# Layer-norm sums on GpSimd: who adds up z and its squares, and who subtracts the mean

## The chip, the cores and the metric

The kernel runs on one core of a Trainium2 chip. The metric is the device time of one execution in microseconds (us); the time before is the median of three executions. The core's engines appear in the profile as PE (TensorE matmuls; PEld its weight loads), DVE (VectorE), ACT (ScalarE), POOL (GpSimd) and SP (SyncE). Each engine works through its own queue in a fixed order; they wait for each other with semaphores.

## What is computed

One inference step of a two-layer decoder trunk, for 256 prompt tokens and 8 sample tokens. In each layer three mixers (retention, a Mamba-2 SSD, sliding-window attention) read the same x, are merged with gates, and go through an output projection; then a SwiGLU FFN. Each half ends in a DeepNorm residual with a layer norm, and it is these norms that the change touches:

```python
def _layer_norm(x, g, b):
    mu = jnp.mean(x, -1, keepdims=True)
    var = jnp.mean(jnp.square(x - mu), -1, keepdims=True)
    return (x - mu) * lax.rsqrt(var + EPS) * g + b

# in each of the DEPTH = 2 layers, D_MODEL = 1024
mix = (g_a * br_a + g_b * br_b + g_c * br_c) @ w_out
x = _layer_norm(ALPHA * x + mix, ln1_g, ln1_b)                 # "norm 1"
ffn = (silu(x @ w_ffn_gate) * (x @ w_ffn_up)) @ w_ffn_down
x = _layer_norm(ALPHA * x + ffn, ln2_g, ln2_b)                 # "norm 2"
```

## The kernel before

**Layout.** All activations stand with channels on the partitions: the 1024 channels are 8 blocks of 128 (KB = 8), and a block is a tile of 128 partitions x 264 columns (T = 264, the 256 + 8 tokens). A projection is a row of units; one unit is one block of 128 output channels, made in one PSUM bank from K = 8 blocks of input.

**Products in three parts.** Full fp32 products are made from fp32r halves: every tensor has a high part and a low part, and for each pair of blocks TensorE multiplies wh by xh, wh by xl and wl by xh (mm3). A unit with K = 8 is so 24 matmuls. The weights arrive as raw strips by DMA on SP's queue and are split here (wsplit, L196): ScalarE copies wh, VectorE subtracts wl = raw - wh (both on 128 x 1024). There are three buffers each of wh and wl, so the splits can be a little ahead of the matmuls.

**The norms.** There are four: norm 1 of layer 0, norm 2 of layer 0, norm 1 of layer 1, and norm 2 of layer 1, which is the last one, has its own code in output() and is not changed ("final"). For block m, residual() makes z[m] from the PSUM result and the high and low part of x in two VectorE steps (the rows z<-xh,ps and z<-xl,z); from block 0 a per-token shift is formed that a matmul with the matrix neg puts into the later blocks. Then residual() does four things with z[m]: VectorE adds it to s1, the sum over blocks (tile s in the rows); ScalarE squares it (sq); the square goes into the sum of squares; and ScalarE and VectorE make the high and low part of g*z (xh and xl) for the next gemm. The sum of squares is kept in two ways. In norm 2 VectorE adds sq to a tile named sums. In norm 1 no such tile is given (sums is None), and TensorE takes every square at once: a product of the 128x128 ones matrix with sq, gathered over eight blocks in the PSUM tile ps_var. Since the matrix is all ones, the product also sums over the 128 partitions and spreads the result to all of them.

ln_stats() finishes the statistics: where sums is given, one product of ones with sums into ps_var; always one product of ones with s1 into ps_mu. ScalarE makes nmu (minus the mean) and the square of the mean, VectorE the variance (the row ps_var<-ps_var,rstd), ScalarE the square root and VectorE the reciprocal: rstd. ln_finish() then normalizes z for all blocks: VectorE adds nmu to z in four steps of two blocks (128x528), scales it by g and rstd, and ScalarE and VectorE make the new high and low part of x.

**What follows a norm.** The next gemms don't wait for ln_finish(). The first 8 units behind a norm run on g*z, not yet normalized (unnormed(), tile ps_z); their results are corrected afterwards by VectorE with nmu, rstd and two more columns of the same gemm (the rows v<-nmu,wc,ps_z). So TensorE can go on while the statistics and the normalized x are being made. Behind norm 1 these are the gemms of FFN blocks f = 0 to 3 (gate and up; w_fg, w_fu); the fifth FFN block is the first to read the normalized x. Behind norm 2 they are layer 1's attention projections (w_qc, w_v and others). The instruction mu_mm, the mean's product, is a mark: the scheduler may not put the later ones of these gemms ahead of it.

**What sets the order.** The code is written against a tile framework with a scheduler that simulates a timeline and decides each engine's order from readiness, priorities (high_priority, for the weight splits and the corrections) and "not before" marks (issue_after). A change of one instruction can so move others on every engine. GpSimd has almost no arithmetic; its queue carries software DMAs (dma(), ld(): parameters, the mixers' states, caches, bias tables) and a few memsets.

## Time and profile before

| what | value |
|---|---|
| time, median of 3 executions | 1091.47 us (1088.8 to 1091.77) |
| the profiled execution's own time | 1088.66 us |
| span of its profile | 1086.9 us |
| PE (TensorE) busy | 1068.3 us, 98% |
| DVE (VectorE) busy | 840.1 us, 77% |
| ACT (ScalarE) busy | 662.4 us, 61% |
| POOL (GpSimd) busy | 163.4 us, 15% |

The profiled execution is one of the kernel's own executions; its span is the time from its first to its last recorded instruction, and 1.8 us of its time lie around that. All times of single instructions are in us from the start of this span. Matmuls are pipelined: a record of 0.28 us starts 0.12 us after the one before it, so the cost of a matmul in a full queue is the distance of starts, not its duration. In a list of waits, a line names the waiting engine with its tile, the engine and tile that released it, and then the sum in us, the number and the mean. In a timeline, what stands in brackets behind a row is the idle time of its engine just before it and who ended it.

In this profile the w_o units of norm 1 in layer 0 run from 331 to 346 us, and the gemms behind it from 347 us on; norm 2 of layer 0 ends near 547 us; norm 1 of layer 1 near 876 us.

### The profile page before, as it was taken

Reading aid. Unit: us, or ns where it says so; the run is one execution under the profiler, and the core shown is the slowest. Engines: PE = TensorE matmul, PEld = TensorE weight load, DVE = VectorE, ACT = ScalarE, POOL = GpSimd, SP = SyncE. Lnnn points to the kernel's source line nnn. Section 1 sums busy time; section 2 is a strip of 40 time slices with the busy share of each in tenths; the row PEclk is TensorE's granted clock in tenths of the full one; section 3 lists DMA queues with packets and bytes.
Section 4 is the critical chain, followed back from the end, with each engine's and each line's share of the span. In section 5 each row is a group of like instructions: output and inputs, shape, how many; then the busy total and the mean of one; then the engine's idle time right before and its main releaser. Section 6 shows DMA issues by size and latency. Waiting matters only on the chain.

```text
span 1086.9 us, 22192 instructions
## 1 busy us (share of the span) xinstructions
PE 1068.3 (98%) x8619; PEld 1029.9 (95%) x8619; DVE 840.1 (77%) x1904; ACT 662.4 (61%) x1332; POOL 163.4 (15%) x248
## 2 busy tenths in 40 slices
PE   9999999999999999999999999999999999999998
PEld 7988998999999999999999899889999999999996
DVE  3588885898868997777599888478886899877654
ACT  3476556667646776665467855366675558666452
POOL 3300012522001011221020001153100000222300
PEclk9999999999999999999999999999999999999999
DMA  9854555994455678899675344669855546989951
GB/s 313 258 175 153 158 145 180 246 273 164 155 194 156 219 247 287 290 312 317 198 254 171 127 156 128 194 160 301 247 183 174 176 149 207 291 286 298 324 183 41
DMA packets 176826, 230.74 MB, mean 212 GB/s; under 512 B 8040, under 2 KB 151984, under 8 KB 176544
## 3 DMA queue, kind: packets, MB, share of 16 engines
q1 hardware_dynamic: 156384, 166.95, 47.6%
q0 software_dynamic: 20272, 62.34, 19.6%
q8 instruction: 68, 1.11, 0.4%
q14 instruction: 38, 0.31, 0.1%
q10 hardware_dynamic: 64, 0.03, 0.0%
HBM read 213.52 MB, written 19.61 MB: 214 GB/s over the span
## 4 chain that ended last, share of the span: by engine, by line
PE 61%; issue 26%; DMA 6%; DVE 3%; POOL 2%; ACT 1%; POOLq 0%; DVEq 0%; ACTq 0%
PE ps_gate L125 12%; PE ps_fg L125 10%; PE ps_fu L125 10%; PE ps_br L125 7%; PE ps_fd L125 6%; PE ps_z L125 5%; PE ps_o L125 4%; PE ps_u L125 4%; DMA bias<-bias_row 2%; DMA rs<-in_state_ret_dram 1%; PE ps_y L125 1%; DVE wl L146 1%; DMA vb<-scr_v 1%; PE ps_var L125 1%; DMA out_dram<-sn 1%
## 5 line engine op out<-in xcount | busy, mean ns | idle before, releaser
L125 PE MATMUL ps_u<-xh,wh 128*128 128x264 f32 x608 | 176.1, 291 | 3.1 <-ACT wh L141 1.8
L125 PE MATMUL ps_u<-xl,wh 128*128 128x264 f32 x608 | 176.4, 290 | 0.0
L125 PE MATMUL ps_u<-xh,wl 128*128 128x264 f32 x608 | 175.6, 291 | 0.1
L125 PEld LDWEIGHTS ps_u<-xh,wh 128*128 128x128 f32 x608 | 116.1, 192 | 6.5 <-ACT wh L141 2.3
L125 PEld LDWEIGHTS ps_u<-xh,wl 128*128 128x128 f32 x608 | 116.5, 192 | 2.1 <-issue 1.7
L125 PEld LDWEIGHTS ps_u<-xl,wh 128*128 128x128 f32 x608 | 116.3, 191 | 1.1 <-issue 0.5
L125 PE MATMUL ps_gate<-xh,wh 128*128 128x264 f32 x384 | 110.1, 290 | 2.2 <-ACT th L141 2.2
L125 PE MATMUL ps_gate<-xl,wh 128*128 128x264 f32 x384 | 109.4, 288 | 0.0
L125 PE MATMUL ps_gate<-xh,wl 128*128 128x264 f32 x384 | 108.9, 288 | 0.0
L125 PE MATMUL ps_fd<-fh,wl 128*128 128x264 f32 x352 | 100.4, 285 | 0.0
L125 PE MATMUL ps_fd<-fh,wh 128*128 128x264 f32 x352 | 100.3, 285 | 0.0
L125 PE MATMUL ps_fd<-fl,wh 128*128 128x264 f32 x352 | 100.0, 284 | 0.0
L125 PE MATMUL ps_fg<-xl,wh 128*128 128x264 f32 x288 | 82.5, 286 | 1.0 <-DVE xl L158 1.0
L169 POOL DMA_DIRECT2D s<-in_state_ssm_dram x32 | 28.8, 900 | 362.4 <-ACT sn L141 229.1
L141 ACT ACTIVATE wh<-w_gate 128x1024 fp32r<-128x1024 f32 x48 | 50.6, 1057 | 53.5 <-PE ps_br L125 19.8
L146 DVE TENSOR_TENSOR wl<-w_fd,wh 128x1024 fp32r<-128x1024 f32 (+1 forms) x48 | 54.2, 1136 | 36.6 <-ACT wh L141 36.5
L125 PE MATMUL ps_fu<-xh,wh 128*128 128x264 f32 x288 | 82.4, 286 | 0.0
L125 PE MATMUL ps_fg<-xh,wh 128*128 128x264 f32 x288 | 82.0, 285 | 0.3 <-DVE v L158 0.3
L125 PE MATMUL ps_fu<-xl,wh 128*128 128x264 f32 x288 | 82.1, 285 | 0.0
L125 PE MATMUL ps_fu<-xh,wl 128*128 128x264 f32 x288 | 81.8, 284 | 0.0
L125 PE MATMUL ps_fg<-xh,wl 128*128 128x264 f32 x288 | 81.7, 284 | 0.0
L141 ACT ACTIVATE wh<-w_fd 128x1024 fp32r<-128x1024 f32 (+1 forms) x48 | 47.1, 986 | 54.8 <-PE ps_fd L125 46.2
(458 smaller groups left out, 3416.0 us busy)
## 6 DMA issues: line engine op xcount, KB each, us to landing
w_gate<-in_w_in_dram SPq DMA_DIRECT2D x24, 1024.0 KB, 5.4
w_fg<-in_w_ffn_gate_dram SPq DMA_DIRECT2D x22, 1024.0 KB, 5.2
w_fu<-in_w_ffn_up_dram SPq DMA_DIRECT2D x22, 1024.0 KB, 6.3
s<-in_state_ssm_dram POOLq DMA_DIRECT2D x32, 512.0 KB, 7.0
w_fd<-in_w_ffn_down_dram SPq DMA_DIRECT2D x16, 1024.0 KB, 8.9
out_dram<-sn POOLq DMA_DIRECT2D x24, 512.0 KB, 7.7
w_qk<-in_w_in_dram SPq DMA_DIRECT2D x8, 1024.0 KB, 9.4
w_xs<-in_w_in_dram SPq DMA_DIRECT2D x8, 1024.0 KB, 5.0
```

The source lines that it names most:

```text
L125: return self.nc.tensor.matmul(out, lhsT, rhs, start=start, stop=stop).ins
L141: i = self.nc.scalar.activation(out=out, in_=in_, func=func, scale=scale, **kw)
L146: return self.nc.vector.tensor_tensor(out=out, in0=a, in1=b, op=op).ins
L169: return self.nc.gpsimd.dma_start(out, in_).ins
```

## The change

A new helper gadd is an addition on GpSimd. In the three norms that aren't final:

- s1 is kept by GpSimd: it starts at block 1 with z[0] + z[1] and takes blocks 2 to 6. Block 7 isn't added.
- the squares are added by GpSimd too, in a tile sums that norm 1 now also has: it begins as block 0's square, blocks 1 to 6 are added, and block 7's square is kept as it is (self.sq).
- ln_stats() makes four products with the ones matrix: of sums into ps_var, of s1 into ps_mu, of z[7] into ps_mu, and of block 7's square into ps_var. The eight products of the squares in each norm 1 are gone.
- ln_finish() adds nmu to z on GpSimd.

```diff
--- before.py
+++ after.py
@@ -151,6 +151,9 @@
     def add(self, out, a, b):
         self.tt(out, a, b, ALU.add)
 
+    def gadd(self, out, a, b):
+        self.nc.gpsimd.tensor_tensor(out=out, in0=a, in1=b, op=ALU.add)
+
     def sub(self, out, a, b):
         self.tt(out, a, b, ALU.subtract)
 
@@ -385,23 +388,22 @@
             if final:
                 self.s1 = self.gp.tile([128, T], F32, tag="s1", bufs=1, name="s1")
                 self.act(self.s1, z[0])
-        elif m == 1:
-            if not final:
-                self.s1 = self.gp.tile([128, T], F32, tag="s1", bufs=1, name="s1")
-            self.add(self.s1, self.s1 if final else z[0], z[1])
-        else:
+        elif m == 1 and not final:
+            self.s1 = self.gp.tile([128, T], F32, tag="s1", bufs=1, name="s1")
+            self.gadd(self.s1, z[0], z[1])
+        elif final:
             self.add(self.s1, self.s1, z[m])
-        if sums is not None:
-            sq = sums if m == 0 else self.gp.tile([128, T], F32, tag="t", name="sq")
-            self.act(sq, z[m], AF.Square)
-            if m:
-                self.add(sums, sums, sq)
-        else:
-            if m == 0:
-                self.pvar = self.pm("ps_var")
-            sq = self.gp.tile([128, T], F32, tag="t", name="sq")
-            self.act(sq, z[m], AF.Square)
-            self.mm(self.pvar[:, :T], self.c("ones"), sq, m == 0, m == KB - 1)
+        elif m < KB - 1:
+            self.gadd(self.s1, self.s1, z[m])
+
+        sq = sums if m == 0 else self.gp.tile([128, T], F32, tag="t", name="sq")
+        self.act(sq, z[m], AF.Square)
+        if final and m:
+            self.add(sums, sums, sq)
+        elif 0 < m < KB - 1:
+            self.gadd(sums, sums, sq)
+        elif m:
+            self.sq = sq
         g = par[:, g0 + m : g0 + m + 1]
         if final:
             self.act(z[m], z[m], AF.Copy, scale=g)
@@ -412,13 +414,13 @@
     def shift(self, ps, first=False):
         self.mm(ps, self.neg, self.z0, first, True)
 
-    def ln_stats(self, sums=None):
-        gp = self.gp
-        if sums is not None:
-            self.pvar = self.pm("ps_var")
-            self.mm(self.pvar[:, :T], self.c("ones"), sums)
-        ps = self.pm("ps_mu")
-        self.mu_mm = self.mm(ps[:, :T], self.c("ones"), self.s1)
+    def ln_stats(self, sums):
+        gp, ones = self.gp, self.c("ones")
+        self.pvar, ps = self.pm("ps_var"), self.pm("ps_mu")
+        self.mm(self.pvar[:, :T], ones, sums, True, False)
+        self.mm(ps[:, :T], ones, self.s1, True, False)
+        self.mu_mm = self.mm(ps[:, :T], ones, self.z[KB - 1], False, True)
+        self.mm(self.pvar[:, :T], ones, self.sq, False, True)
         nmu = self.nmu = gp.tile([128, T], F32, tag="s1", bufs=1, name="nmu")
         r = self.rstd = gp.tile([128, T], F32, tag="z0", bufs=1, name="rstd")
         v = self.pvar[:, :T]
@@ -433,7 +435,7 @@
         par, g0 = self.lnp
         for k0 in range(0, KB, 2):
             zb = self.zt[:, k0 * T : (k0 + 2) * T].rearrange("p (k t) -> p k t", k=2)
-            self.add(zb, zb, self.nmu.unsqueeze(1).to_broadcast([128, 2, T]))
+            self.gadd(zb, zb, self.nmu.unsqueeze(1).to_broadcast([128, 2, T]))
             split = k0 in (6,)
             if split:
                 self.mul(zb, zb, self.rstd.unsqueeze(1).to_broadcast([128, 2, T]))
@@ -714,6 +716,7 @@
             self.stt(lo, mix[m], 0.5, h.bitcast(F32), ALU.mult, ALU.subtract)
             mx.append((h, lo))
         self.ln_start(l, 0)
+        sums = self.E1("sums")
         wo = a["w_out"][l].rearrange("(k p) c -> p k c", p=128)
         for s in range(4):
             raw = self.strip([(0, 128, wo[:, :, s * 256 : s * 256 + 256])], (8, 256), "w_o")
@@ -724,10 +727,10 @@
                 self.gemm(w, mx, ps[:, :T], last=m == 0)
                 if m:
                     self.shift(ps[:, :T])
-                self.residual(m, ps[:, :T], None)
+                self.residual(m, ps[:, :T], sums)
         if l + 1 < DEPTH:
             self.params(l + 1)
-        self.ln_stats()
+        self.ln_stats(sums)
 
     def branch(self, l, gi, kk, loads, gens, hl, parts=(0, 1), between=None):
 
```

The scheduler makes these orders of it. In the names, w_o is norm 1's projection, xh and xl are the high and low part of x (in a norm: of g*z), s_ and a number is s1, cst is the table with the ones matrix.

**Norm 1 of layer 0, TensorE.** Before, among the matmuls of the late w_o units (mh and ml are the high and low part of their input; two blocks' squares stand five rows apart):

```order
L125 MATMUL ps_var<-sq,cst 128x264
L125 MATMUL ps_o<-mh,wl 128x264
L125 MATMUL ps_o<-mh,wh 128x264
L125 MATMUL ps_o<-ml,wh 128x264
L125 MATMUL ps_o<-mh,wl 128x264
L125 MATMUL ps_var<-sq,cst 128x264
L125 MATMUL ps_o<-mh,wh 128x264
L125 MATMUL ps_o<-ml,wh 128x264
```

After, all of the norm's statistics products stand behind the last w_o unit, in the gemm on the unnormalized z (ps_z, 128x266 with the two extra columns); the first of the four and the two that follow:

```order
L125 MATMUL ps_z<-xh,wh 128x266
L125 MATMUL ps_var<-sums,cst 128x264
L125 MATMUL ps_mu<-s_4185,cst 128x264
L125 MATMUL ps_z<-xl,wh 128x266
L125 MATMUL ps_z<-xh,wl 128x266
L125 MATMUL ps_mu<-z,cst 128x264
L125 MATMUL ps_z<-xh,wh 128x266
```

The products of single squares have left the w_o units; the fourth new one, ps_var<-sq, stands six matmuls further on.

**The same norm, GpSimd.** Before, between the parameter loads and the loads of the SSD state (vb is a broadcast row):

```order
L169 DMA par_rows<-in_d_skip_dram 1x16x1
L169 DMA par_rows<-in_sinks_dram 1x8x1
L169 DMA s_4851<-in_state_ssm_dram 128x8x128
L169 DMA vb<-scr_bc 128x256
L169 DMA s_4855<-in_state_ssm_dram 128x8x128
```

After:

```order
L172 DMA par_rows<-in_sinks_dram 1x8x1
L155 ISA
L155 TENSOR_TENSOR s_4185<-z 128x264
L155 TENSOR_TENSOR s_4185<-s_4185,z 128x264
L155 TENSOR_TENSOR sums<-sums,sq 128x264 x2
L155 TENSOR_TENSOR s_4185<-s_4185,z 128x264
L155 TENSOR_TENSOR sums<-sums,sq 128x264
L155 TENSOR_TENSOR s_4185<-s_4185,z 128x264 x2
L155 TENSOR_TENSOR sums<-sums,sq 128x264 x2
L155 TENSOR_TENSOR s_4185<-s_4185,z 128x264
L155 TENSOR_TENSOR sums<-sums,sq 128x264
L172 DMA s_4851<-in_state_ssm_dram 128x8x128
```

The twelve adds stand in GpSimd's queue ahead of the first state load. The row ISA is an instruction that comes with GpSimd's arithmetic.

**Norm 2 of layer 0, VectorE.** Before, the last three blocks, the variance, the subtraction of the mean, and the reciprocal (w_qc is a projection of layer 1):

```order
L146 TENSOR_TENSOR s_6578<-s_6578,z_6242 128x264
L146 TENSOR_TENSOR sums<-sums,sq 128x264
L158 SCALAR_TENSOR_TENSOR xl<-z_6242,par_410,xh 128x264
L158 SCALAR_TENSOR_TENSOR z_6242<-xl,z_6242 128x264
L146 TENSOR_TENSOR s_6578<-s_6578,z_6242 128x264
L146 TENSOR_TENSOR sums<-sums,sq 128x264
L158 SCALAR_TENSOR_TENSOR xl<-z_6242,par_410,xh 128x264
L846 MEMSET dtac 128x48
L158 SCALAR_TENSOR_TENSOR ps_var<-ps_var,rstd 128x264
L146 TENSOR_TENSOR z_6242<-z_6242,nmu 128x528 x4
L472 RECIPROCAL rstd<-rstd 128x264
L146 TENSOR_TENSOR wl<-w_qc,wh 128x1024
```

After:

```order
L161 SCALAR_TENSOR_TENSOR xl<-z_6242,par_410,xh 128x264
L161 SCALAR_TENSOR_TENSOR z_6242<-xl,z_6242 128x264
L146 TENSOR_TENSOR wl<-w_qc,wh 128x1024
L161 SCALAR_TENSOR_TENSOR z_6242<-xh,ps_fd 128x264
L161 SCALAR_TENSOR_TENSOR xl<-z_6242,par_410,xh 128x264
L161 SCALAR_TENSOR_TENSOR z_6242<-xl,z_6242 128x264
L161 SCALAR_TENSOR_TENSOR xl<-z_6242,par_410,xh 128x264
L849 MEMSET dtac 128x48
L161 SCALAR_TENSOR_TENSOR ps_var<-ps_var,rstd 128x264
L146 TENSOR_TENSOR wl<-w_qc,wh 128x1024
L474 RECIPROCAL rstd<-rstd 128x264
L161 SCALAR_TENSOR_TENSOR v<-nmu,wc,ps_z 128x264
```

The adds into s_6578 and sums are gone from between the steps of z, and a split of w_qc has come into the place of the subtraction z<-z,nmu.

**The same norm, GpSimd.** Before, the loads for layer 1 stand alone (the convolution's rows, the bias tables, a key cache, the retention states rs):

```order
L169 DMA cst_rows<-in_state_conv_dram 24x1536
L169 DMA bias_t<-bias 128x4x256 x2
L169 DMA kcache<-in_cache_swa_k_dram 128x8x128
L1217 MEMSET qz 128x256
L1218 MEMSET qn 128x128
L835 MEMSET dt 128x48
L169 DMA rs_8545<-in_state_ret_dram 128x8x128
L169 DMA rs_8756<-in_state_ret_dram 128x8x128
```

After, with the last adds ahead of them:

```order
L155 TENSOR_TENSOR s_6578<-s_6578,z_6242 128x264
L155 TENSOR_TENSOR sums<-sums,sq 128x264
L172 DMA w_dt<-in_w_in_dram 128x8x16
L172 DMA cst_rows<-in_state_conv_dram 24x1536
L172 DMA bias_t<-bias 128x4x256 x2
L172 DMA kcache<-in_cache_swa_k_dram 128x8x128
L1220 MEMSET qz 128x256
L1221 MEMSET qn 128x128
L838 MEMSET dt 128x48
L172 DMA rs_8545<-in_state_ret_dram 128x8x128
L172 DMA rs_8756<-in_state_ret_dram 128x8x128
L155 TENSOR_TENSOR z_6242<-z_6242,nmu 128x528 x4
```

The loads now stand behind the last two adds, and the four subtractions of the mean behind the loads.

## Rows read from the trace of the kernel before

**Rows 1.** The page's busy times over the span, by engine:

```profile
PE 1068.3 (98%) x8619; PEld 1029.9 (95%) x8619; DVE 840.1 (77%) x1904; ACT 662.4 (61%) x1332; POOL 163.4 (15%) x248
```

**Rows 2.** TensorE's list of waits: who waits, releaser, then us, times, mean:

```profile
PE ps_fg L125 <- DVE xl L158: 1.0, 1, 1.0
PE ps_z L125 <- ACT xh L141: 0.7, 1, 0.7
PE ps_fg L125 <- DVE v L158: 0.3, 1, 0.3
```

**Rows 3.** Busy time by stretch: length, engines' busy us (instructions), clock, DMA share, GB/s:

```profile
326.00:346.00 20.00, 20.00 (x155) 19.39 (x153) 18.41 (x35) 12.57 (x22) 0.00 (x0) 1.00 0.48 158
346.00:376.00 30.00, 29.03 (x227) 28.38 (x226) 27.78 (x48) 24.29 (x51) 2.97 (x4) 1.00 0.70 209
...
543.00:575.00 32.00, 31.16 (x250) 29.59 (x250) 30.75 (x65) 21.94 (x49) 7.33 (x13) 1.00 0.78 254
850.00:876.00 26.00, 26.00 (x202) 25.34 (x201) 21.16 (x40) 15.50 (x26) 0.00 (x0) 1.00 0.38 122
876.00:906.00 30.00, 29.68 (x235) 29.12 (x234) 29.42 (x55) 20.66 (x44) 0.00 (x0) 1.00 0.59 191
```

The engines stand in the order PE, PEld, DVE, ACT, POOL.

**Rows 4.** Timeline of TensorE in a w_o unit: start, duration, instruction:

```profile
332.41 0.28 PE L125 MATMUL ps_o<-ml,wh 128*128 128x264 f32 x1
332.53 0.61 PE L125 MATMUL ps_var<-sq,cst 128*128 128x264 f32 x2
332.79 0.48 PE L125 MATMUL ps_o<-mh,wl 128*128 128x264 f32 x1
333.10 0.28 PE L125 MATMUL ps_o<-mh,wh 128*128 128x264 f32 x1
```

**Rows 5.** Instructions on ps_var and ps_mu: count, ns min/median/max, first to last start:

```profile
L125 PE MATMUL ps_var<-sq,cst x32: 383/386/490, 332.5 to 876.4; 128*128 128x264 f32 x32
...
L125 PE MATMUL ps_var<-sums,cst x2: 383/384/384, 548.0 to 548.2; 128*128 128x264 f32 x2
...
L125 PE MATMUL ps_mu<-s,cst x6: 383/386/388, 349.7 to 876.8; 128*128 128x264 f32 x6
```

**Rows 6.** Timeline of TensorE at norm 2 of layer 0:

```profile
546.17 0.28 PE L125 MATMUL ps_z<-xh,wh 128*128 128x266 f32 x1
...
546.83 0.28 PE L125 MATMUL ps_z<-xh,wl 128*128 128x266 f32 x1
547.80 0.39 PE L125 MATMUL ps_z<-xh,wh 128*128 128x266 f32 x1 [0.69 <-ACT xh L141]
```

**Rows 7.** Timeline of VectorE at norm 2 of layer 0:

```profile
545.36 0.43 DVE L146 TENSOR_TENSOR s<-s,z 128x264 f32<-128x264 f32 x1
545.71 0.43 DVE L146 TENSOR_TENSOR sums<-sums,sq 128x264 f32<-128x264 f32 x1
...
546.46 0.43 DVE L158 SCALAR_TENSOR_TENSOR z<-xl,z 128x264 f32<-128x264 f32 x1
```

**Rows 8.** Timeline of VectorE, the subtraction of the mean at norm 2:

```profile
549.89 2.56 DVE L146 TENSOR_TENSOR z<-z,nmu 128x528 f32<-128x528 f32 x4
```

**Rows 9.** Timeline of ScalarE, the first high part of normalized x behind norm 2:

```profile
569.73 0.90 ACT L141 ACTIVATE xh<-z,par 128x264 fp32r<-128x264 f32 x2
```

**Rows 10.** Timelines of VectorE and of GpSimd in output(), near the end:

```profile
1078.81 1.61 DVE L158 SCALAR_TENSOR_TENSOR yt<-ps_y,stat,br 128x512 f32<-128x512 f32 x2
...
1079.66 1.27 POOL L1622 TENSOR_TENSOR yt<-yt,br 128x512 f32<-128x512 f32 x1 [49.65 <-ACT yt L141]
```

**Rows 11.** Timeline of GpSimd behind norm 1 and at norm 2 of layer 0:

```profile
346.32 0.98 POOL L169 DMA_DIRECT2D s<-in_state_ssm_dram  x1 [93.99 <-PE ps_par L129]
...
544.27 0.52 POOL L169 DMA_DIRECT2D cst_rows<-in_state_conv_dram  x1 [8.56 <-PE ps_fd L125]
```

**Rows 12.** Timelines of VectorE and TensorE, a split of w_o and its unit's matmul:

```profile
336.06 1.23 DVE L146 TENSOR_TENSOR wl<-w_o,wh 128x1024 fp32r<-128x1024 f32 x1
...
342.06 0.28 PE L125 MATMUL ps_o<-mh,wh 128*128 128x264 f32 x1
```

## The prediction, made before the changed kernel ran

> **What bounds the kernel now.** I read the page's busy times first: TensorE is busy 1068 of 1087 us, VectorE 840 [rows 1]. TensorE is the bound, so a thing is worth what it takes from TensorE's own queue or from the moments in which that queue stands still. The list of TensorE's waits comes next; three of its entries lie at the three norms that the change touches: ps_fg waiting for xl (1.0 us, after norm 1 of layer 0), ps_z waiting for xh (0.7 us, norm 2 of layer 0), ps_fg waiting for v (0.3 us, after norm 1 of layer 1) [rows 2]. Then the busy time by stretch: around these norms VectorE is nearly full as well, 18.4 of 20 and 27.8 of 30 us at the first, 30.8 of 32 after the second, 29.4 of 30 after the third; only ahead of the third it has room, 21.2 of 26 [rows 3]. So at the norms two engines are close to the bound, and the change gives work to a third and takes some from both. The granted clock is 1.00 in all these stretches, the upper level (2.4 GHz), so no term below is one of the clock.
>
> **Products on TensorE.** A statistics product against the 128x128 ones matrix is two records. In the row of matmuls at 332 us an ordinary one starts 0.12 us before the next (332.41 to 332.53). From the start of the product at 332.53 to the second start behind it at 333.10 are 0.57 us, which hold the product and one ordinary matmul, so the product costs 0.57 - 0.12 = 0.45 us [rows 4]. There are 32 + 2 + 6 records, so 20 products in three norms [rows 5]: 9 in each norm 1 (eight squares and one mean), 2 in norm 2. After, every norm has 4: 12 in all. Taken away: 8 x 0.45 = **3.6 us**, namely 2.25 at each norm 1, less 0.9 added at norm 2. TensorE is busy there without a hole, so nothing hides these and nothing else has to become faster for the gain to appear, as long as no wait fills the place.
>
> **VectorE's share.** It loses 7 adds in each norm 1 and 14 in norm 2, 28 in all; queued back to back one takes 0.35 us (545.36 to 545.71) [rows 7], together 9.8 us. It loses the four subtractions of each norm, 2.56 us a set [rows 8], together 7.7. Sum 17.5 us, none of it on TensorE's chain by itself; it counts where VectorE is late. That is plain at norm 2: the three matmuls from 546.17 on should have been out by 546.54, but the next one starts at 547.80, a loss of 1.26 us, because the last block of z was held up on VectorE [rows 6]. In its queue that block's second step, at 546.46, follows two sum adds (545.36 and 545.71) that are no longer there [rows 7]. Without them the step and the xh behind it come 0.7 us earlier. The last block doesn't pass through the sums any more either: TensorE takes it straight from z. Against that, the first product now waits for GpSimd's sums of seven blocks. I therefore count half of the loss, **0.6 us**. The 1.0 and 0.3 us after the norms 1 I leave where they are: VectorE stays full there.
>
> **GpSimd's share.** It gets 12 adds of 128x264 and 4 subtractions of 128x528 in each norm. The only two-operand row on GpSimd is 128x512 in 1.27 us [rows 10]; in proportion 264 columns are 0.66 us and 528 are 1.31. 36 x 0.66 + 12 x 1.31 = 40 us, for the 17.5 taken from VectorE. In time it fits: a norm 1 has eight blocks of 24 matmuls, so one about every 24 x 0.12 = 2.9 us, and two adds take 1.3. Is GpSimd free otherwise? Before the state loads behind norm 1 of layer 0 it stands idle for 94 us, and those loads were held until 346.32 anyway, so the adds ahead of them delay nothing; the library instruction before the first add falls into the same idle time [rows 11]. At norm 2 the loads that stood at 544.27 and after now follow the adds, whose last must come after the seventh block's square, near 546. They shift by some 2 us, and the four subtractions, which follow these loads in GpSimd's queue, begin near 552.5 instead of 549.89 and end near 558 instead of 552.5 [rows 8, 11]. Who waits for that: VectorE's scaling of z by rstd, which in the new order stands behind three more weight splits and a reciprocal, near 556, when the first pair is done. And xh of the normed x was made only at 569.73 [rows 9]; these 10 us hide it. I cost all this at nothing; if the cover went, it would be up to 5 us, once.
>
> **What the trace doesn't show** is what GpSimd's reads do to VectorE. The one add on GpSimd, at 1079.66, ran beside VectorE instructions that take an operand from PSUM, two of them in 1.61 us: no slowing that can be seen, but neither has two operands in SBUF [rows 10]. The weight splits and most steps of z have two. So GpSimd's 40 us cost VectorE between 0 and 40 us. VectorE breaks even at 17.5/40 = 44%. I take that share, neither gain nor loss, since the nearest row shows no slowing and the splits are of another kind.
>
> The Trainium skill, SBUF — State Buffer, section Who interferes with whom, has a rule against this change: a VectorE instruction with two SBUF inputs and a GpSimd instruction that reads SBUF share one read interface, and the second to start waits until the first has ended. No run here shows it. By that rule the sum would be that of the second rival below, or of the third where nearly every add hits such an instruction.
>
> **Sum.** 3.6 + 0.6 = 4.2 us. Against the profiled execution's 1088.66 us (span 1086.9) that is 1084.5. The median of the runs shown is 1091.47, 2.8 above it; on that scale the forecast is 1091.47 - 4.2 = **1087.3 us**.
>
> **Rivals.**
> 1. All three waits go too (chance 0.10): VectorE is 17.5 us freer and GpSimd costs it little. 3.6 + 1.26 + 1.0 + 0.3 = 6.2 us, 1085.3. For it: the lighter queue at norm 2. Against: VectorE has hardly any idle time after the norms in which to get ahead.
> 2. The gain is eaten (0.26): GpSimd blocks VectorE for some 63% of its time, the share of a block's 2.9 us that VectorE spends on two-operand instructions (a split 1.2, a step of z and xl some 0.6). 0.63 x 40 - 17.5 = 7.7 us more for VectorE over three norms, while TensorE comes 3.6 us earlier: 11 us to find. VectorE's idle time in the five stretches is 1.6 + 2.2 + 1.25 + 4.8 + 0.6 = 10.5 us [rows 3], but not all of it falls where it is needed. The waits grow by about 3 us and take the products' gain: near 1090.8.
> 3. VectorE becomes the bound at the norms (0.18, the slower one): nearly every add stops a weight split for its whole length. At a share of 80% VectorE has 32 - 17.5 = 14.5 us more to do. The splits are ahead of TensorE: the last one of w_o ended at 337.29 and its matmuls began at 342.06, 4.8 us later [rows 12]. Once that lead is used up, TensorE waits for wl. 14.5 less the 10.5 idle, plus the 3.6 by which TensorE comes earlier, is 7.6 us of new waits; less the 3.6 of the products, 4 us slower, and more where the idle time lies badly: 1096. It decides from a share of 70%, where the waits reach 3.6 us.
> That the change does not do what it says can be ruled out: the order has the products gone and the adds on GpSimd. Smaller is that layer 1's small products of SWA, retention and SSD stand some units later after the move; waits of TensorE there can shift by one or two us either way, which the range carries.
>
> **How the numbers follow.** Forecast 0.46, rivals 0.10, 0.26 and 0.18. A measurement of this kernel tells 0.3%, 3.3 us, from no change, so faster is below 1088.2 and slower above 1094.7. The forecast's own spread (1084.5 to 1089.5) puts 0.37 of its 0.46 below 1088.2; with the first rival, 0.47 faster. Within: 0.33, the rest of the forecast and most of the second rival. Slower: 0.20, the third and a little of the second. The range of 8 in 10 is 1083.5 to 1094.0: it leaves out the best of the first rival and the upper part of the third.
>
> **What would show it.** Right: 24 records of statistics products at the three norms instead of 40; ps_z no longer waiting 0.7 us at norm 2; GpSimd adds near 0.66 us; the splits beside them still 1.2 us. Wrong: GpSimd adds well over 1 us, splits beside them at 1.5 us or more, TensorE waiting for wl, for the sums from GpSimd, or for xl in the fifth block of the FFN longer than 1.0 us. If the splits keep 1.2 us and no wait appears and the time is still 1090 or more, the products were not on the path, and the first step failed.

## The result: slower by 0.8%

| | before | after |
|---|---|---|
| time, median | 1092.03 us (8 executions, 1088.80 to 1098.78) | 1101.82 us (8 executions, 1098.02 to 1104.39) |
| ratio after / before | | 1.0076, 95% interval 1.0048 to 1.0105 |
| span of the profile | 1086.9 us | 1101.0 us |

The change costs 5 to 11 us. I had forecast 1087.3 us and a range up to 1094.0. The page's busy times of the kernel after stand against [rows 1]:

```profile
PE 1071.1 (97%) x8603; PEld 1032.2 (94%) x8603; DVE 842.2 (76%) x1864; ACT 664.7 (60%) x1334; POOL 222.5 (20%) x296
```

TensorE has 16 instructions less, as the change says, and yet 2.8 us more of busy time; a second profile of the kernel before has 1070.5, so 2.2 of that is no more than what two executions of one kernel differ by. VectorE lost 40 instructions and isn't less busy (842.2 against 840.1). GpSimd has 59 us more. The records of the statistics products (instructions on ps_var and ps_mu, to be read beside [rows 5]) are 24 instead of 40:

```profile
L125 PE MATMUL ps_var<-sums,cst x6: 386/438/490, 351.4 to 884.7; 128*128 128x264 f32 x6
L125 PE MATMUL ps_var<-sq,cst x6: 383/386/387, 353.9 to 887.4; 128*128 128x264 f32 x6
...
L125 PE MATMUL ps_mu<-s,cst x6: 386/386/386, 352.0 to 885.1; 128*128 128x264 f32 x6
L125 PE MATMUL ps_mu<-z,cst x6: 383/384/387, 352.7 to 886.0; 128*128 128x264 f32 x6
```

TensorE's list of waits, in the columns of [rows 2], shows what came in their place:

```profile
PE ps_fg L125 <- DVE v L161: 3.1, 2, 1.9
PE ps_y L125 <- DVE L L146: 3.0, 2, 2.5
PE ps_gate L125 <- ACT th L141: 3.0, 2, 1.8
...
PE ps_var L125 <- POOL sums L155: 2.5, 3, 1.3
...
PE ps_br L125 <- DVE yhl L146: 2.0, 2, 1.5
...
PE ps_fu L125 <- DVE v L161: 1.3, 1, 1.3
```

The three waits for sums are the three norms: TensorE stands until GpSimd has added the seventh block. The waits for v lie behind the norms 1. The longest waits for L, th and yhl (the SSD's decay matrix, a gate and the SSD's output) lie in the mixers of layer 1, where the diff touches nothing. The one for L is new; the other two have grown, as the same list of the kernel before says:

```profile
PE ps_gate L125 <- ACT th L141: 2.2, 2, 1.1
...
PE ps_br L125 <- DVE yhl L146: 1.0, 2, 0.5
```

**Stage by stage.** To see where the spans part I cut both at TensorE's first matmul on ps_o (the w_o units begin; before, that is at 318.71 us, not near 331), on ps_fd (the FFN's down projection) and on ps_u (layer 1's mixers). In the kernel after these are, in the timeline's columns:

```profile
322.82 0.28 PE L125 MATMUL ps_o<-mh,wh 128*128 128x264 f32 x1
...
482.81 0.28 PE L125 MATMUL ps_fd<-fh,wh 128*128 128x264 f32 x1
...
576.83 0.52 PE L125 MATMUL ps_u<-xh,wh 128*128 128x264 f32 x2
...
856.07 0.28 PE L125 MATMUL ps_o<-mh,wh 128*128 128x264 f32 x1
...
1019.35 0.28 PE L125 MATMUL ps_fd<-fh,wh 128*128 128x264 f32 x1
```

The table gives the length of each stage before in us, and for every other kernel of this study the difference to it. "Norm 1" runs from the first w_o matmul to the first of ps_fd, "norm 2" from there to the first of ps_u.

| profile of | ahead of w_o | norm 1, layer 0 | norm 2 | layer 1's mixers | norm 1, layer 1 | rest |
|---|---|---|---|---|---|---|
| before | 318.71 | 160.06 | 93.90 | 273.19 | 158.92 | 82.12 |
| before, once more | +4.24 | -0.01 | +0.03 | -0.48 | -0.05 | +1.07 |
| **after** | +4.11 | -0.07 | +0.12 | **+6.05** | **+4.36** | -0.47 |
| norm 2 as before | +4.02 | -0.05 | +0.01 | -0.61 | +4.27 | +1.16 |
| norms 1 as before | +2.24 | -0.01 | +0.12 | +3.97 | -0.07 | -0.45 |
| subtraction on VectorE | +0.55 | -1.39 | +0.83 | +0.81 | +0.03 | +4.07 |
| sums on VectorE | +0.17 | +0.17 | +0.25 | +0.57 | +1.03 | +2.21 |
| all on VectorE | +6.10 | +2.49 | +1.01 | +1.54 | +1.05 | +1.21 |
| sums on GpSimd, norms 1 only | +0.93 | -1.40 | 0.00 | +0.75 | +0.06 | +6.06 |
| squares on GpSimd, norms 1 only | +4.26 | +4.07 | +0.04 | -0.74 | +1.09 | +0.08 |
| additions left out, norms 1 only | +1.79 | -2.09 | +0.03 | +0.87 | -2.22 | +5.92 |
| mean first, norms 1 only | +2.25 | -1.87 | +0.03 | +1.68 | -0.65 | +1.16 |
| norm 2, three subtractions | +4.81 | -0.03 | +0.75 | -0.30 | -0.06 | -0.37 |
| probe (norms as before) | +5.19 | +0.47 | +0.03 | +1.85 | -0.06 | +1.07 |

The first and the last column are no work of the change: ahead of w_o every kernel has the same order on TensorE, VectorE and ScalarE, and the same kernel profiled twice gives 318.71 and 322.95 there. That is chance of one execution, and the profile of before that I worked from is at its short end. In the two profiles of the kernel before, the three norm stages repeat to 0.05 us. Layer 1's mixers repeat less well: they last 272.5 to 275.0 us in all kernels that keep the old order there or nearly so (the 275.0 is the probe, whose order there is that of before), and 277.2 and 279.2 in the two with the new one. Part of this spread is TensorE's clock, which is granted at the lower level (1.2 GHz) for part of this stage: that takes 1.7 us in the kernel before, nothing in the run "norm 2 as before", 3.4 us in the probe. So a single profile prices this stage to some 2 us only. Read that way, the kernel after loses about 6 us in layer 1's mixers and 4.4 at norm 1 of layer 1, and nothing at the other two norms, where the products alone had promised a gain of 2.25 us at norm 1 of layer 0 and a loss of 0.9 at norm 2. The sum, 10.5, lies within the measured 5 to 11.

### The profile page after: what moved, and what is told of

Same layout as the page of the kernel before. It is cut to its first block, busy times and chain, and to the rows that moved or that the text cites. A ratio compares the mean times of both kernels' runs of the same rounds, so it can differ in the third digit from the quotient of the medians.

```text
span 1101.0 us, 22225 instructions
## 1 busy us (share of the span) xinstructions
PE 1071.1 (97%) x8603; PEld 1032.2 (94%) x8603; DVE 842.2 (76%) x1864; ACT 664.7 (60%) x1334; POOL 222.5 (20%) x296
## 3 DMA queue, kind: packets, MB, share of 16 engines
q8 instruction: 68, 1.11, 0.4%
## 4 chain that ended last, share of the span: by engine, by line
PE 68%; issue 13%; DVE 7%; DMA 6%; ACT 3%; POOL 2%; POOLq 0%; ACTq 0%; DVEq 0%
PE ps_fd L125 11%; PE ps_gate L125 10%; PE ps_fg L125 10%; PE ps_fu L125 9%; PE ps_u L125 9%; PE ps_br L125 7%; PE ps_z L125 4%; DVE wl L146 2%; DMA s<-in_state_ssm_dram 2%; PE ps_o L125 2%; DMA bias<-bias_row 2%; ACT wh L141 1%; DVE z L161 1%; DVE xl L161 1%; PE ps_y L125 1%
## 5 line engine op out<-in xcount | busy, mean ns | idle before, releaser
L125 PEld LDWEIGHTS ps_gate<-xh,wh 128*128 128x128 f32 x384 | 73.0, 190 | 4.1 <-ACT th L141 3.3
```

The costliest lines, as they stand in the source:

```text
L125: return self.nc.tensor.matmul(out, lhsT, rhs, start=start, stop=stop).ins
```

## Experiments

Two causes were to be told apart: theory A, that GpSimd and VectorE hold each other up at the norms 1 and that norm 2's change made the scheduler arrange layer 1's mixers anew; against it that all of the loss is the one or all of it the other.

**Norm 2 as before** (the norms 1 changed). A flag chooses the code of before:

```diff
+        self.old = which == 1
...
-            self.gadd(self.s1, z[0], z[1])
+            (self.add if self.old else self.gadd)(self.s1, z[0], z[1])
...
+        elif (final or self.old) and m:
             self.add(sums, sums, sq)
...
-            self.gadd(zb, zb, self.nmu.unsqueeze(1).to_broadcast([128, 2, T]))
+            (self.add if self.old else self.gadd)(zb, zb, self.nmu.unsqueeze(1).to_broadcast([128, 2, T]))
```

> The two norms 1 as in the changed kernel, norm 2 of layer 0 as in the kernel before (sums and subtraction on VectorE, two products). TensorE's order in layer 1's mixers is then nearly that of before. Theory A (two causes: GpSimd and VectorE hold each other up at the norms 1, and norm 2's change rearranged layer 1's mixers): in the two profiles the norms 1 moved TensorE by -0.1 and +4.4 us net, so about +4 us against before, near 1096, with waits for the sums and for v at the norms 1, and no new waits between 700 and 830 us. Rival B (the whole loss is layer 1's new order; the norms give their 4.5 us of products back as forecast): 4 us faster than before, near 1088. Rival C (the whole loss is at the norms): +9, near 1101.

Measured: 1098.02 us, ratio 1.0045 (1.0022 to 1.0069). The mixers are as before (-0.6), the norms 1 give -0.05 and +4.27, as in the kernel after to 0.1 us.

**Norms 1 as before** (norm 2 changed): the same with `which == 0`.

> Only norm 2 of layer 0 is changed; both norms 1 are as before. Layer 1's mixers stand in the order of the changed kernel. Theory A: norm 2 itself costs nothing that can be seen, layer 1's mixers cost about 6 us by new waits between 700 and 830 us (for L of the SSD, 2.5 us and more, and a clock at the lower level behind it): near 1098. Rival B (all of it is the order): +9, near 1101. Rival C (all at the norms, the order neutral): within 2 us of before, near 1092.

Measured: 1094.51 us, ratio 1.0028 (1.0005 to 1.0050). Norms 1 as before, norm 2 +0.12, the mixers +3.97 (about 6 were expected), with a wait for L of 2.6 us. The two losses are separate and add up: 0.45% and 0.28% against 0.76% for both. Rivals B and C fall.

**Subtraction on VectorE**, the sums still on GpSimd:

```diff
-            self.gadd(zb, zb, self.nmu.unsqueeze(1).to_broadcast([128, 2, T]))
+            self.add(zb, zb, self.nmu.unsqueeze(1).to_broadcast([128, 2, T]))
```

> As the changed kernel, with the subtraction of the mean back on VectorE; the sums stay on GpSimd. Layer 1's mixers come out nearly in the order of before. Theory A: the 4 us in which a split of w_fg stood still beside GpSimd's subtractions are gone, the wait for v behind norm 1 of layer 1 falls from 3.2 us to under 1, the wait for the sums stays (0.9 and 1.3 us): -1 to +2 us against before, near 1092. Rival D (the sums do the harm, not the subtraction): the waits behind the norms 1 stay, +4, near 1096.

Measured: 1095.17 us, ratio 1.0035 (1.0014 to 1.0057), slower than expected. The stages did what theory A says: -1.39 and +0.03 at the norms 1, the waits for v gone, the wait for the sums still there. But the last stage is 4.1 us longer: in it a strip of w_fd lands late, and TensorE waits 2.8 us. That wait is in four of the profiles and not in the others; whether it belongs to these kernels or to the execution stays open. One of the four is the run without additions below, whose profiled execution (1093.0 us) is the slowest of its eleven, which suggests that most of its executions go without it. For this run the norms and the mixers give +0.3 us of a median that is 3.8 us higher; the rest is not explained.

**Sums on VectorE**, the subtraction on GpSimd:

```diff
-            self.gadd(self.s1, self.s1, z[m])
+            self.add(self.s1, self.s1, z[m])
...
-            self.gadd(sums, sums, sq)
+            self.add(sums, sums, sq)
```

> As the changed kernel, with the sums back on VectorE (blocks 0 to 6, the last by TensorE as in the change); the subtraction stays on GpSimd. Theory A: the wait of ps_var for the sums goes, the long split beside the subtractions stays (over 3 us), so does a wait for v behind norm 1 of layer 1: +1 to +4, near 1094. Rival D (the sums do the harm): 3 us faster than before, near 1089.

Measured: 1094.07 us, ratio 1.0032 (1.0013 to 1.0051): in theory A's range, but not for its reasons. The wait for the sums didn't go, it changed its owner: TensorE waits 1.09 and 1.62 us for VectorE's sums, more than for GpSimd's. And the long split beside the subtractions, with the wait for v behind norm 1 of layer 1, didn't stay: TensorE's list has no wait for v there, and of VectorE's splits beside the four subtractions the longest is

```profile
881.12 1.97 DVE L146 TENSOR_TENSOR wl<-w_fg,wh 128x1024 fp32r<-128x1024 f32 x1 [0.88 <-ACT wh L141]
```

It began beside the second subtraction and got in when that one ended.

**A probe of the two engines.** In the FFN of layer 0, where the splits are well ahead, GpSimd gets work that nobody uses:

```diff
+        gp.tensor_tensor(out=d, in0=h, in1=lo, op=ALU.add)
+        for _ in range(6):
+            if kind == "add":
+                gp.tensor_tensor(out=d, in0=h, in1=lo, op=ALU.add)
+            elif kind == "copy":
+                gp.tensor_copy(out=d, in_=h)
+            else:
+                gp.memset(d, 0.0)
```

> The kernel before, with extra work for GpSimd in the FFN of layer 0 that nothing uses: in blocks 6 to 8 seven additions of two SBUF tiles (128x264) each, in blocks 10 to 12 one addition and six copies, in blocks 14 to 16 one addition and six memsets of the same size. The orders of TensorE, VectorE and ScalarE are those of before. Theory A (a VectorE instruction with two operands in SBUF and a GpSimd instruction that reads SBUF exclude each other): beside the additions and the copies some splits of w_fg and w_fu last 1.5 to 2.0 us instead of 1.22, some GpSimd instructions last about a split longer than their shortest, and beside the memsets every split keeps 1.22. Rival E (they only share bandwidth): all of them are stretched a little, memsets too, and no single one waits for a whole other instruction. TensorE has room there (the splits are ahead), so the time stays within 0.3% of before.

Measured: one execution of 1097.2 us, within the spread of the kernel before on that chip (1087.3 to 1100.2), but 0.6% above its median, so that one execution neither bears out nor refutes the 0.3%. The instructions on the probe's tile, in the columns of [rows 5]:

```profile
L1579 POOL TENSOR_TENSOR probe<-fh,fl x18: 743/766/1822, 403.0 to 431.6; 128x264 f32<-128x264 f32 x18
L1581 POOL COPY probe<-fh x18: 409/414/1470, 437.6 to 463.2; 128x264 f32<-128x264 f32 x18
L1583 POOL MEMSET probe<- x18: 318/320/343, 472.5 to 484.2; 128x264 f32 x18
```

And three moments of its timeline, GpSimd's row ahead of VectorE's:

```profile
421.57 0.77 POOL L1579 TENSOR_TENSOR probe<-fh,fl 128x264 f32<-128x264 f32 x1
...
421.65 1.78 DVE L149 TENSOR_TENSOR wl<-w_fg,wh 128x1024 fp32r<-128x1024 f32 x1
...
424.63 1.63 POOL L1576 TENSOR_TENSOR probe<-fh,fl 128x264 f32<-128x264 f32 x1
...
424.22 1.42 DVE L149 TENSOR_TENSOR wl<-w_fu,wh 128x1024 fp32r<-128x1024 f32 x1
...
475.65 2.20 POOL L1583 MEMSET probe<- 128x264 f32 x6
...
475.69 1.22 DVE L149 TENSOR_TENSOR wl<-w_fu,wh 128x1024 fp32r<-128x1024 f32 x1
```

At 421.57 the addition was first and keeps its 0.77 us; the split that started 0.08 later lasts 1.78: the 0.69 that were left of the addition and 1.09 more, nearly its own 1.22. The split at 424.22 was ahead of the addition at 424.63, which lasts 1.63 for it (the split itself lasts 1.42, since an earlier addition was still running when it began). Copies, with one operand, show the same (414 ns, longest 1470). Memsets keep 318 to 343 ns, and the split beside the first of six keeps 1.22. It is a whole exclusion, not a sharing, and it needs a read on GpSimd's side: rival E falls. This is the rule of the Trainium skill (SBUF — State Buffer, section Who interferes with whom) that the prediction quoted as speaking against the change; in this probe the trace agrees with it. (The last section has a case in which the instruction that was first to wait was not the first to get in.)

**Before once more**, unchanged code.

> The kernel before, unchanged: a second profile of the same code. Before the first w_o unit and behind the last FFN of layer 1 the changed kernel differs from before in no order on TensorE, yet its profile was 4.1 us later there by the first w_o unit. If that is chance of an execution, this profile's first w_o matmul starts anywhere between 317 and 323 us (before: 318.7); the stages from there to layer 1's last FFN are the same as in the first profile to 0.5 us.

Measured: 1093.54 us, one execution; its stages are the table's second row. As expected.

**Sums on GpSimd, norms 1 only**: norm 2 as before, all subtractions on VectorE.

```diff
+        self.old = which == 1
...
-            self.gadd(zb, zb, self.nmu.unsqueeze(1).to_broadcast([128, 2, T]))
+            self.add(zb, zb, self.nmu.unsqueeze(1).to_broadcast([128, 2, T]))
```

> Norms 1 with the sums on GpSimd and the last block by TensorE, but the subtraction on VectorE; norm 2 as before. Theory A: the stages as in the run with the subtraction on VectorE at the norms 1 (-1.4 and 0.0 us), layer 1's mixers and norm 2 as in the kernel before: -1 to -2 us, near 1089.5. Rival D (the sums on GpSimd do the harm): +1 to +3, near 1093.

Measured: 1091.75 us, ratio 1.0002 (0.9978 to 1.0026). The norms 1 give -1.40 and +0.06, as expected; in the whole no difference can be told. Against the kernel after, the subtraction's price beside sums on GpSimd is therefore 1.3 us at norm 1 of layer 0 (-0.07 against -1.40) and 4.3 at that of layer 1.

**Squares on GpSimd, norms 1 only**: z's own sum stays on VectorE, eight blocks as before.

```diff
+        if sums is not None and self.sqg:
+            sq = sums if m == 0 else self.gp.tile([128, T], F32, tag="t", name="sq")
+            self.act(sq, z[m], AF.Square)
+            if 0 < m < KB - 1:
+                self.gadd(sums, sums, sq)
+            elif m:
+                self.sq = sq
...
-                self.residual(m, ps[:, :T], None)
+                self.residual(m, ps[:, :T], sums)
```

> Norms 1 with only the squares on GpSimd (six additions, the last square by TensorE); z's own sum and the subtraction stay on VectorE, norm 2 as before. The products fall from 9 to 3, 2.7 us less for TensorE at each norm 1. Theory A: six additions hold VectorE up by 0 to 5 us at each norm, half as many as with both sums, so the wait for the sums falls below 0.8 us: 1 to 3 us faster than before, near 1089. Rival F (VectorE is so full there that losing its seven additions mattered more): waits for xl and v behind the norms 1 grow by the 2.5 us that those additions take, +1, near 1092.

Measured: 1097.24 us, ratio 1.0056 (1.0028 to 1.0083): wrong by theory A, and more than rival F had. Half the additions on GpSimd, and +4.07 and +1.09 at the norms 1. The wait for the sums did fall (0.40 and 0.38 us). TensorE's list of waits says what is late now:

```profile
PE ps_z L125 <- DVE xl L161: 2.6, 3, 1.1
...
PE ps_fg L125 <- DVE xl L161: 2.1, 3, 1.2
```

Of the +4.07 the clock is the larger part. Behind two of these waits at norm 1 of layer 0 the granted clock falls (columns as [rows 3]):

```profile
352.00:357.00 5.00, 3.88 (x16) 3.24 (x15) 4.43 (x8) 1.50 (x4) 2.47 (x4) 0.69 0.65 131
380.00:385.00 5.00, 4.88 (x25) 4.61 (x26) 5.00 (x13) 3.62 (x10) 0.00 (x0) 0.66 0.66 209
```

That takes (0.31 + 0.34) x 5 = 3.3 us, where the kernel before loses nothing. The seven additions of z stood in VectorE's queue before, too; GpSimd's six beside them are new, and one of the seven at each norm 1 now lasts 0.99 or 0.98 us instead of 0.43. That VectorE's queue at the norm counts more than GpSimd's is the reading that fits; no run separates it from TensorE's coming earlier.

**Norm 2 with three of its four subtractions on GpSimd**, norms 1 as before. With this the scheduler keeps nearly the old order of layer 1's mixers, while GpSimd does all additions and three quarters of the subtraction:

```diff
+        self.old = which == 0
...
-            self.gadd(zb, zb, self.nmu.unsqueeze(1).to_broadcast([128, 2, T]))
+            (self.gadd if not self.old and k0 // 2 in [0, 1, 2] else self.add)(zb, zb, self.nmu.unsqueeze(1).to_broadcast([128, 2, T]))
```

> Only norm 2 of layer 0 is changed, and there all twelve additions and three of the four subtractions are on GpSimd; the fourth is on VectorE. TensorE's order in layer 1's mixers is then nearly that of before (some 130 rows differ, instead of some 2100 with the fourth on GpSimd too). Theory A (the loss in layer 1's mixers comes from the order, which the scheduler chose anew): that stage lasts 272.5 to 274 us as before, no wait for L of the SSD, 0 to +1 us in all, near 1091. Rival G (it comes from GpSimd's work at norm 2, by late loads or a late x): the stage lasts 276.5 us or more, +3 to +4, near 1094.

Measured: 1092.39 us, ratio 1.0001 (0.9979 to 1.0023), the mixers at 272.89 us. Rival G falls: the loss in the mixers isn't GpSimd's work at norm 2 as such, it is the order (that the fourth subtraction alone did it in another way, no run excludes). The place shows it too. Busy time by stretch, columns as [rows 3], of the kernel after:

```profile
790.00:795.00 5.00, 4.37 (x38) 3.83 (x36) 5.00 (x17) 5.00 (x14) 0.00 (x0) 1.00 0.64 211
795.00:800.00 5.00, 3.10 (x15) 2.47 (x16) 5.00 (x13) 1.48 (x5) 0.00 (x0) 0.63 0.61 211
800.00:805.00 5.00, 5.00 (x31) 5.00 (x30) 3.84 (x11) 1.06 (x1) 0.00 (x0) 0.69 0.01 3
```

and of this run, in the same stage:

```profile
790.00:800.00 10.00, 10.00 (x82) 9.93 (x82) 7.50 (x13) 6.38 (x9) 0.00 (x0) 1.00 0.66 219
800.00:805.00 5.00, 4.88 (x40) 4.68 (x39) 5.00 (x11) 4.98 (x10) 0.00 (x0) 1.00 0.02 9
```

GpSimd does nothing there in either. In the kernel after VectorE is full, TensorE waits 2.54 us for L, and behind the wait the granted clock is 0.63 and 0.69: the lower level for part of the time, which costs (0.37 + 0.31) x 5 = 3.4 us of TensorE's work.

**Additions left out** at the norms 1 (blocks 2 to 6 are in no sum, so this prices the products without any adder):

```diff
-        elif m < KB - 1:
-            self.gadd(self.s1, self.s1, z[m])
...
         elif 0 < m < KB - 1:
-            self.gadd(sums, sums, sq)
+            pass
```

> Norm 2 as before. At the norms 1 four products as in the change, the subtraction on VectorE, and the additions of blocks 2 to 6 are left out altogether (nobody adds them: sums holds block 0's square alone, s1 blocks 0 and 1). Theory A (the products lay on TensorE's path, and what gives them back are the adders): w_o's stage is 2.9 us shorter at each norm 1, the stage behind it 0 to 1 us longer, 4 to 5.5 us faster in all, near 1086. Rival H (the products were hidden anyway): within 1 us of before, near 1091.

Measured: 1088.03 us, ratio 0.9948 (0.9923 to 0.9973), and -2.09 and -2.22 at the norms 1. Five products less at each were priced at 2.25. Rival H falls: the products were on the path. The run frees VectorE of seven additions at each norm 1 as well, and the waits for xl and v there fall by 0.25 and 0.31 us; what is left for the products is some 1.9 us of the 2.25.

**Mean first**, as the run with the sums on GpSimd at the norms 1 only, with the two products of the mean ahead of those of the squares:

```diff
+            self.mm(ps[:, :T], ones, self.s1, True, False)
+            self.mu_mm = self.mm(ps[:, :T], ones, self.z[KB - 1], False, True)
+            with self.tc.issue_after(self.mu_mm):
+                self.mm(self.pvar[:, :T], ones, sums, True, False)
+                self.mm(self.pvar[:, :T], ones, self.sq, False, True)
```

> As the run with the sums on GpSimd at the norms 1 only, and TensorE takes the two products of the mean first and the two of the squares behind them. Theory A: TensorE's wait for the sums (0.85 and 1.35 us there) falls below 0.4 each, the rest of the stages stays: 2 to 3 us faster than before, near 1088. Rival I (VectorE's xl is the next in line): the wait only changes its name, as that run, near 1091.

Measured: 1090.70 us, ratio 0.9978 (0.9955 to 1.0001), -1.87 and -0.65 at the norms 1. In the middle between theory A and rival I. It has the lowest ratio of the versions that compute everything, at the edge of what can be told from no change; its interval overlaps that of the run with the sums on GpSimd at the norms 1 only. The wait for the sums is gone from TensorE's list; part of it has changed its name:

```profile
PE ps_mu L125 <- POOL s L155: 1.2, 2, 0.8
...
PE ps_z L125 <- DVE xl L161: 0.4, 1, 0.4
PE ps_mu L125 <- DVE z L161: 0.3, 1, 0.3
```

**All on VectorE**: the edits of the two runs "sums on VectorE" and "subtraction on VectorE" together.

> The four products of the change at all three norms, but every addition and subtraction on VectorE; GpSimd does none of them. VectorE gets five more additions at each norm 1 (1.75 us) and loses two at norm 2. Theory A (VectorE is full at the norms 1, whoever blocks it): TensorE waits 1 to 1.6 us for the sums at each norm 1 as in the run with the sums on VectorE, but no longer for v: 0 to 2 us faster than before, near 1090. Rival D (GpSimd alone did the harm): 4 us faster, near 1087.

Measured: 1097.09 us, ratio 1.0043 (1.0013 to 1.0072): slower than theory A had, and the opposite of rival D. TensorE waits for the sums (1.11 and 1.62 us), and then still for xl:

```profile
PE ps_var L125 <- DVE sums L146: 2.7, 2, 1.6
PE ps_fg L125 <- DVE xl L161: 2.4, 2, 1.4
```

And behind the wait for xl at norm 1 of layer 0 the granted clock falls here, too:

```profile
378.00:384.00 6.00, 5.10 (x27) 4.92 (x28) 6.00 (x16) 5.11 (x12) 0.00 (x0) 0.72 0.55 176
```

0.28 x 6 = 1.7 us of that stage's +2.49 are the clock.

So who adds, in us at the two norms 1 with the subtraction on VectorE: nobody -2.09 and -2.22; GpSimd -1.40 and +0.06; VectorE +2.49 and +1.05. With the subtraction on GpSimd it is GpSimd -0.07 and +4.36, VectorE +0.17 and +1.03. The two moves aren't independent: GpSimd is the better place for the sums as long as it doesn't subtract as well, and beside sums on VectorE the subtraction on GpSimd costs nothing at norm 1 of layer 1 (+1.03 against +1.05).

## Why the prediction was wrong, point by point

**The products: right, to within a fifth.** 3.6 us were forecast, 2.25 at each norm 1 less 0.9 at norm 2. The run without additions gives 2.1 and 2.2 at the norms 1, some 1.9 of it by the products.

**GpSimd's durations: nearly right alone, wrong in place.** I had 0.66 us for an addition and 1.31 for a subtraction. Not held up, they are 0.77 (the probe's median; 43 us in all instead of 40) and 1.30 (four back to back in 5.19 us, below). In place the groups of GpSimd say:

```profile
L155 POOL TENSOR_TENSOR sums<-sums,sq 128x264 f32<-128x264 f32 x18 | 19.7, 1096 | 0.3 <-ACT sq L141 0.2
L155 POOL TENSOR_TENSOR z<-z,nmu 128x528 f32<-128x528 f32 x12 | 18.4, 1565 | 0.0
L155 POOL TENSOR_TENSOR s<-s,z 128x264 f32<-128x264 f32 x15 | 18.0, 1203 | 26.2 <-DVE z L161 26.1
```

With the three of block 1 (3.3 us) that is 59 us: the waiting for VectorE stands in the durations.

**VectorE's share: right, and of no use.** I set its loss to exclusion at 44% of GpSimd's 40 us, 17.5, which is just what it is relieved of. It was relieved of 17.5 and is 2.1 us busier, so the loss was 19.6, or 49%. The share was a choice, so its closeness is luck: of the two VectorE instructions of [rows 10] that I took it from, only the second (1079.67, 0.75 us) ran beside GpSimd's addition at all. And I took a sum of VectorE's time that comes out even for a path that comes out even. What matters is which instruction is held up. At norm 1 of layer 1, in the kernel after (VectorE, then GpSimd):

```profile
891.16 4.31 DVE L146 TENSOR_TENSOR wl<-w_fg,wh 128x1024 fp32r<-128x1024 f32 x1
895.40 0.48 DVE L161 SCALAR_TENSOR_TENSOR v<-nmu,wc,ps_z 128x264 f32<-128x264 f32 x1
...
889.19 5.19 POOL L155 TENSOR_TENSOR z<-z,nmu 128x528 f32<-128x528 f32 x4
```

The split stands still for 3.1 us, until the last of the four subtractions is over, and behind it in VectorE's queue stands the first v, on which the FFN's hidden blocks and in the end a PSUM bank depend. From there to 912 us VectorE has no idle time in which to catch up. At norm 1 of layer 0 the same four met mostly the reciprocal, which is not held up (1.80 us there as in the kernel before), and cost 1.3 us instead of 4.3. The step that failed is "I take that share, neither gain nor loss": with it the sum held no new wait of TensorE behind the norms 1 ("the 1.0 and 0.3 us after the norms 1 I leave where they are"), and the first product's wait for GpSimd's sums was set off at norm 2 only. In its place stand these rows of TensorE in the kernel after:

```profile
884.37 0.49 PE L125 MATMUL ps_var<-sums,cst 128*128 128x264 f32 x1 [1.31 <-POOL sums L155]
...
909.50 0.36 PE L125 MATMUL ps_fu<-xh,wh 128*128 128x264 f32 x1 [1.34 <-DVE v L161]
...
911.73 0.36 PE L125 MATMUL ps_fg<-xh,wh 128*128 128x264 f32 x1 [1.86 <-DVE v L161]
```

4.5 us of idle time instead of 0.3. And behind them the clock falls, in a sum that had no term of the clock:

```profile
910.00:915.00 5.00, 3.27 (x15) 3.15 (x16) 5.00 (x13) 4.04 (x10) 0.00 (x0) 0.74 0.53 173
915.00:920.00 5.00, 5.00 (x39) 5.00 (x39) 4.61 (x12) 2.00 (x5) 0.00 (x0) 0.92 0.72 226
```

(0.26 + 0.08) x 5 = 1.7 us more. With 2.25 for the products taken off, 4.2 + 1.7 - 2.25 = 3.65 of the stage's 4.36; each pause also costs somewhat more than its idle time, as at norm 2 before, where the 1.26 us that were lost [rows 6] hold 0.69 of idle time ahead of one matmul and 0.15 ahead of an earlier one.

**Norm 2: right.** The wait for xh is gone, a wait for the sums of 0.31 us and two more products have come: I had 0.9 - 0.6 = +0.3, the stage is +0.12. The cover for the late subtraction held: that is what "I cost all this at nothing" was said of.

**Layer 1's order: named, and mis-sized.** I gave the moved mixers "one or two us either way". They cost 4.0 us alone and 6.0 in the kernel after, in one profile each, and so to some 2 us. In the latter TensorE's waits there sum to 7.3 us against 4.2 before, and two stretches at the lower clock to 1.7 + 3.4 us against 1.7. The clock's part is not the new order's alone, since the probe loses 3.4 to it with the old one. The places for it were in the comparison of the two orders: more than half of TensorE's 2200 matmuls of that stage stand in another order (some 2% with three subtractions), and I priced none. This second term was mis-sized by 2 to 5 us.

**The rivals.** The third had the sign, at less than half of the loss (4 us of some 10), and not the mechanism: TensorE doesn't wait for weight splits (0.2 us for wl in all). What comes late is what stands behind a held instruction: v and xl on VectorE, and the sums on GpSimd. The second, a gain that is eaten, is what norm 1 of layer 0 shows (-0.07 instead of -2.25).

**The scale.** I set the sum against a profile whose stage ahead of w_o is 4 us shorter than in the second one of the same code. The median of runs absorbed that; the difference of the two spans, 14.1 us, doesn't, and is too large by those 4 us.

## What to carry to other kernels

Here the 17.5 us that were moved from a nearly full VectorE to an idle GpSimd came back as 19.6 us of waiting, because both read SBUF. Count what stands behind the instruction that is held up, not the engines' sums. A change of a few instructions under a scheduler is also a change of everything that it rearranges: compare the orders outside of the edit, and try a neighbour of the edit that leaves them alone. And cut the profile into stages that can be compared: here the norm stages repeat to 0.05 us where whole executions differ by ten; and look at the granted clock of each, which took 1.7 or 3.4 us of TensorE's work wherever it fell in these stages.

## What the runs showed of the hardware

The exclusion isn't always in turn. Four subtractions on GpSimd in a row (5.19 us, 1.30 each) kept a split waiting from 891.16 to about 894.3 (it ends at 895.47 and needs 1.22), though the second and the third of them ended in between; in the run "norm 2 as before" the same split lasts 4.27 us in the same place. Elsewhere the waiting instruction gets in as soon as the one ahead of it ends. At norm 2 of the kernel after, a split begins beside the second subtraction, and it is the third that waits:

```profile
559.27 1.61 DVE L146 TENSOR_TENSOR wl<-w_qc,wh 128x1024 fp32r<-128x1024 f32 x1
...
559.77 2.30 POOL L155 TENSOR_TENSOR z<-z,nmu 128x528 f32<-128x528 f32 x1
```

The split of 1.97 us with the sums on VectorE is another such case. What decides between the two, no run shows; at norm 1 of layer 1 it goes with the whole difference between a wait for v and none. And the profile doesn't mark the exclusion: an engine that is locked out shows as busy, with an instruction of 4.31 us instead of 1.22.
